# Low halves of weight tiles by an adding transfer instead of a VectorE subtraction, for two tiles of every eight

## The chip, the cores and the metric

The kernel runs on one core of one Trainium2 chip. The metric is the device time of one execution in microseconds. A core has a matrix engine (TensorE, PE in the profile), VectorE (DVE), ScalarE (ACT), GpSimd (POOL) and SyncE (SP), each with an instruction queue of its own that is worked through in order, and sixteen DMA engines that move data between DRAM and the on-chip memory, or within the latter. Instructions of different engines wait for one another by semaphores. A DMA can be issued from SP's, ScalarE's or GpSimd's queue.

## The reference

A trunk of two layers over 256 tokens of 2048 features, float32. Layer 0 mixes tokens with an mLSTM (8 heads), layer 1 with a Griffin block (convolution of width 4 and a gated linear recurrence). After each mixer comes a feed-forward block with 5632 inner features, and a final norm ends it:

```python
for layer in range(DEPTH):
    hn = rms_norm(h, norm_mix[layer])
    mix = mlstm_mixer(...) if layer % 2 == 0 else rglru_mixer(...)
    h = h + mix
    h = h + swiglu(rms_norm(h, norm_ffn[layer]), ffn_w_in[layer], ffn_w_out[layer])
return rms_norm(h, norm_final)
```

What matters here is only that nearly all the work is products `x @ w` of 256 tokens with large weight matrices: the mixers' input and output projections, and `ffn_w_in` (2048 x 11264) and `ffn_w_out` (5632 x 2048) of each layer. Every weight is used once.

## The kernel before, in words

The products must have nearly float32 precision. TensorE multiplies in a faster 32-bit format that keeps fewer bits (float32r). So each weight and each activation is split in two: a high half, which is the value rounded to float32r, and a low half, which is the value minus its high half. A product is then high x high + high x low + low x high.

The weights come in tiles of 256 rows x 512 columns (512 KB): 128 partitions, two row blocks, `NB` = 512 columns. `load_raw` (its DMA is line 77 of the profile) issues the load of such a tile on SP's queue into the buffer `raw`. The generator `stream` then has ScalarE copy `raw` into `whi`, rounding to float32r (line 161), and VectorE subtract `whi` from `raw` into `wlo` (line 162). It yields the row blocks one after the other to the product loops `linear_tok` (products in lines 176 to 178), `linear_feat` (through `mm_feat`, lines 193 to 195) and `linear_wide` (lines 217 and 218); in all of them the product with `wlo` is the second or third of a row block. A whole run has 752 such tiles: 96 of `m_w_in`, 32 of `m_w_out`, 352 of `ffn_w_in`, 176 of `ffn_w_out`, 64 of `r_w_in` and 32 of `r_w_out`. The first four tiles are loaded ahead of the program (`raw0`; the first of them in two halves); `stream` calls these `first`.

`raw`, `whi` and `wlo` each have four buffers (`wpool`, `bufs=4`): a buffer is written anew when all readers of the tile four places before are done. The scheduler orders each engine's instructions by priority; the split runs under `tc.high_priority(offset=AHEAD)`, so that it is placed as early as the buffers allow:

```python
with tc.high_priority(offset=0 if first else AHEAD):
    for i in range(0, 2, step):
        r = raw[:, i:i + step, 0:ncols]
        nc.scalar.copy(hi[:, i:i + step, 0:ncols], r)
        nc.vector.tensor_tensor(lo[...], r, hi[...].bitcast(F32), op=ALU.subtract)
```

The eight gate weight tiles of layer 1 (`gr`, loaded in line 614) share the `raw`, `whi` and `wlo` buffers and are split by `split_store` (lines 318 and 319).

GpSimd has little to do: 62 instructions, among them the reciprocal roots of the norms (line 291) and of the mLSTM heads (line 489), the scaling of the heads (line 490), and in the last feed-forward the product of h with the final gain (line 698). It issues no DMA. The results of one phase are worked on by the other engines between the products of the next (`pending`, `run_pending`).

Of the kernel before, what the change touches and what calls it, by code (L numbers as in the profile page):

```python
# [11 lines left out]
ALU = mybir.AluOpType  # L12
PSUM = bass.MemoryType.PSUM

P = 128
T = 256
# [15 lines left out]
def kernel(  # L32
# [21 lines left out]
    nc = tc.nc  # L54
# [10 lines left out]
    def misc(name):  # L65
        return ps_m.tile([P, NB], F32, tag="misc", name=name)

# [1 line left out]
    h = const.tile([P, NT, D], F32, name="h")  # L69
    xv = x[0].rearrange("(b p) d -> p b d", p=P)  # L70
    raw0 = {}
# [12 lines left out]
                for kg in (4 * q, 4 * q + 2):  # L84
                    raw0[kg] = load_raw(m_w_in[0], 0, NB, kg, 1 if kg == 0 else 2)

# [1 line left out]
    ident = const.tile([P, P], F32, name="ident")  # L88
    make_identity(nc, ident)
    ones = const.tile([P, P], F32, name="ones")  # L90
    nc.vector.memset(ones, 1.0)
    warm = const.tile([P, 1], F32, name="warm")
    nc.scalar.activation(warm, ones[:, 0:1], AF.Exp)
    # the tensor engine's clock rises only while it works
    pwarm = misc("warm")
    for i in range(12):
        nc.tensor.matmul(pwarm[:, 0:P], lhsT=ones, rhs=ones, start=(i == 0), stop=(i == 11))
# [6 lines left out]
        pattern=[[1, P]], channel_multiplier=-1,  # L104
    )

# [1 line left out]
    par_src = [  # L108
        ("g_mix", norm_mix.rearrange("l (k p) -> (l k) p", p=P), 32),
        ("g_ffn", norm_ffn.rearrange("l (k p) -> (l k) p", p=P), 32),  # L110
# [7 lines left out]
    rows = [const.tile([P, P], F32, name=f"rows{i}") for i in range(3)]  # L118
# [20 lines left out]

    par_cols(0)  # L140

# [1 line left out]
    pending = []  # L143

    def run_pending():
        if pending:
            pending.pop(0)()

# [1 line left out]
    def stream(w, c0, nk, ncols=NB):  # L150
        """Yields (k, hi, lo) for the 128-row tiles of w[:, c0:c0+ncols]."""
        for kg in range(0, nk, 2):
            first = kg in raw0
            raw = raw0.pop(kg) if first else load_raw(w, c0, ncols, kg)
            hi = wpool.tile([P, 2, NB], F32R, tag="whi", name=f"whi{kg}")
            lo = wpool.tile([P, 2, NB], F32R, tag="wlo", name=f"wlo{kg}")
            step = 1 if first and kg == 0 else 2
            with tc.high_priority(offset=0 if first else AHEAD):
                for i in range(0, 2, step):
                    r = raw[:, i:i + step, 0:ncols]  # L160
                    nc.scalar.copy(hi[:, i:i + step, 0:ncols], r)  # L161
                    nc.vector.tensor_tensor(  # L162
                        lo[:, i:i + step, 0:ncols], r, hi[:, i:i + step, 0:ncols].bitcast(F32), op=ALU.subtract
                    )
            for i in range(2):
                yield kg + i, hi[:, i, 0:ncols], lo[:, i, 0:ncols]

    def linear_tok(w, c0, nk, act, name, ncols=NB, lag=0):
        """[tokens, ncols] in PSUM, one tile for each block of 128 tokens."""
        ps = [acc(f"{name}_{b}") for b in range(NT)]  # L170

        def block(b, k, hi, lo):
            ah, al = act(k)
            bs = slice(b * P, (b + 1) * P)
            o = ps[b][:, 0:ncols]
            nc.tensor.matmul(o, lhsT=ah[:, bs], rhs=hi, start=(k == 0), stop=False)  # L176
            nc.tensor.matmul(o, lhsT=ah[:, bs], rhs=lo, start=False, stop=False)  # L177
            nc.tensor.matmul(o, lhsT=al[:, bs], rhs=hi, start=False, stop=(k == nk - 1))  # L178

        late = []  # L180
        for k, hi, lo in stream(w, c0, nk, ncols):
            block(0, k, hi, lo)
            late.append((k, hi, lo))
            if len(late) > lag:
                block(1, *late.pop(0))
            if k > 1:
                run_pending()
        for kt in late:
            block(1, *kt)
        return ps  # L190
# [4 lines left out]
        nc.tensor.matmul(o, lhsT=lo, rhs=ah, start=False, stop=last, skip_group_check=True)  # L195

    def linear_feat(w, c0, nk, act, name):
        """[features, tokens] in PSUM: two tiles of two blocks of 128 features."""
        ps = [acc(f"{name}_{b}").rearrange("p (f t) -> p f t", f=2) for b in range(2)]
        for k, hi, lo in stream(w, c0, nk):  # L200
            ah, al = act(k)
            for f in range(4):
                fs = slice(f * P, (f + 1) * P)
                mm_feat(ps[f // 2][:, f % 2, :], hi[:, fs], lo[:, fs], ah, al,
                        k == 0 and f % 2 == 0, k == nk - 1)
            if k > 1:
                run_pending()
        return ps

    def linear_wide(w, c0, nk, act, act2, name):  # L210
        """Four tiles of 128 features: columns 0:T and T:2T are to be added to get [features, tokens]."""
        ps = [acc(f"{name}_{f}") if f < 2 else misc(f"{name}_{f}") for f in range(4)]
        for k, hi, lo in stream(w, c0, nk):
            ah, _ = act(k)
            for f in range(4):
                fs = slice(f * P, (f + 1) * P)
                nc.tensor.matmul(ps[f], lhsT=hi[:, fs], rhs=act2(k), start=(k == 0), stop=False, skip_group_check=True)  # L217
                nc.tensor.matmul(ps[f][:, 0:T], lhsT=lo[:, fs], rhs=ah, start=False, stop=(k == nk - 1),  # L218
                                 skip_group_check=True)
            if k > 1:  # L220
                run_pending()
        return ps
# [6 lines left out]
    def bc4(ap):  # L229
        return ap.unsqueeze(1).broadcast_to([P, 4, T])  # L230

# [1 line left out]
    class Norm:  # L233
        lag = 0

# [66 lines left out]
        return ap.unsqueeze(1).broadcast_to([P, 2, T])  # L302

    def project_out(w, nk, act, nxt):
        """h += act.T @ w, and the next norm's operands, by quarters."""
        for q in range(4):
            ps = linear_tok(w, q * NB, nk, act, f"po{q}", lag=nxt.lag if q == 3 else 0)
            for b in range(NT):
                hs = h[:, b, q * NB:(q + 1) * NB]
                nc.vector.tensor_tensor(hs, ps[b], hs, op=ALU.add)  # L310
                if q == 3 and nxt.lag:
                    nxt.store(b)
            if q < 3 or not nxt.lag:
                pending.append(lambda q=q: nxt.done(q))

    def split_store(dst_hi, dst_lo, src):
        """The two halves of src (SBUF or PSUM), of the same shape."""
        nc.scalar.copy(dst_hi, src)
        nc.vector.tensor_tensor(dst_lo, src, dst_hi.bitcast(F32), op=ALU.subtract)

    def log1p_exp_nabs_half(pool, xin, shape, name):
        """log1p(exp(-|x|)) / 2, by the series of atanh."""
        e = pool.tile(shape, F32, name=f"{name}_e", tag=f"{name}_e", bufs=1)
        nc.scalar.activation(e, xin, AF.Abs)
        nc.scalar.activation(e, e, AF.Exp, scale=-1.0)
        s = pool.tile(shape, F32, name=f"{name}_s", tag=f"{name}_s", bufs=1)
# [5 lines left out]
        p = pool.tile(shape, F32, name=f"{name}_p", tag=f"{name}_p", bufs=1)  # L332
# [3 lines left out]
        nc.vector.scalar_tensor_tensor(out=p, in0=p, scalar=1.0, in1=s, op0=ALU.add, op1=ALU.mult)  # L336
        return p

    # =============================== layer 0: mLSTM ===============================
    n0 = Norm("m0", par["g_mix"][:, 0:16], bcast=True)  # L340
    for q in range(4):
        n0.quarter(q)
# [2 lines left out]
    def mlstm_mixer():  # L345
        with tc.tile_pool(name="mx", bufs=2) as mx:
            w = m_w_in[0]
            sel = mx.tile([H, H, P], F32R, name="sel", bufs=1)
            nc.gpsimd.tensor_copy(sel, ident[0:H, 0:H].unsqueeze(2).broadcast_to([H, H, P]))
            # gates  # L350
            gw = mx.tile([P, NK, 2 * H], F32, name="gw", bufs=1)
            nc.sync.dma_start(gw, w.rearrange("(k p) n -> p k n", p=P)[:, :, 6144:6160])
            gwx = mx.tile([P, NK, 2, 2 * H], F32R, name="gwx", bufs=1)
# [27 lines left out]
            def gate_rows():  # L381
# [9 lines left out]
                nc.vector.tensor_scalar_min(fg, fg, 0.0)  # L391
                lf = fg
                nc.vector.scalar_tensor_tensor(out=lf, in0=lp, scalar=-2.0, in1=fg, op0=ALU.mult, op1=ALU.add)
                # sums of log forget gates and running maxima, in blocks of 128 tokens
                cs = mx.tile([H, T], F32, tag="lf_e", name="cs", bufs=1)
                one8 = ones[0:H, :]
                for b in range(NT):
# [21 lines left out]

            pending.append(gate_rows)  # L420

            # q and k, features on partitions
            qT = mx.tile([P, H, T], F32, name="qT", bufs=1)
            kT = mx.tile([P, H, T], F32, name="kT", bufs=1)
            pw = []
# [84 lines left out]
            for j in range(4):  # L510
# [18 lines left out]
                hi = mx.tile([P, 4, T], F32R, tag=f"yh{j}", name=f"yh{j}", bufs=1)  # L529
                lo = mx.tile([P, 4, T], F32R, tag=f"yl{j}", name=f"yl{j}", bufs=1)  # L530
# [5 lines left out]

    mlstm_mixer()

    # =============================== feed-forward ===============================
    def ffn(layer, n, nxt):  # L540
        with tc.tile_pool(name=f"ff{layer}", bufs=2) as fp:
            w = ffn_w_in[layer]
# [19 lines left out]
    n2 = Norm("m1", par["g_mix"][:, 16:32], bcast=True)  # L562
    ffn(0, n1, n2)

    # =============================== layer 1: RG-LRU ===============================
    # 8 * softplus(-a)
    ap = par["a"]
    lpa = log1p_exp_nabs_half(const, ap, [P, NK], "spa")
    sp8 = const.tile([P, NK], F32, name="sp8")
# [7 lines left out]
    def rglru_mixer():  # L577
        with tc.tile_pool(name="rg", bufs=1) as rg:
            w = r_w_in[0]
# [26 lines left out]

            def gates(j):
                rv, rvh, rvl = rvs[j], rvhs[j], rvls[j]
                # gates of the two blocks of 256 channels
                r = rg.tile([P, 4, T], F32, tag="r", name=f"r{j}")  # L610
                ii = rg.tile([P, 4, T], F32, tag="ii", name=f"ii{j}")
                for g in range(2):
                    raw = wpool.tile([P, 2, NB], F32, tag="raw", name=f"gr{j}{g}")
                    nc.sync.dma_start(raw, gwv[:, 4 * j + 2 * g:4 * j + 2 * g + 2, :])
                    hi = wpool.tile([P, 2, NB], F32R, tag="whi", name=f"ghi{j}{g}")
                    lo = wpool.tile([P, 2, NB], F32R, tag="wlo", name=f"glo{j}{g}")
                    split_store(hi, lo, raw)
                    for half, dst in ((0, r), (1, ii)):
# [6 lines left out]
                        for f in range(2):  # L625
# [1 line left out]
                            nc.scalar.activation(  # L627
                                dst[:, 2 * g + f, :], pg[:, f, :], AF.Sigmoid, bias=par["gb"][:, gb:gb + 1]
                            )
                # log a = -8 softplus(-a) r;  1 - a^2 = tanh(-log a) (1 + a^2)  # L630
                th = rg.tile([P, 4, T], F32, tag="th", name=f"th{j}")
                for f in range(4):
                    k = 4 * j + f
# [49 lines left out]

    rglru_mixer()

    # =============================== last feed-forward, final norm ===============================
    class Final(Norm):
        lag = 4

# [62 lines left out]
```

## Time and profile before

| | |
|---|---|
| median of 2 runs | 2186.55 us |
| the two runs | 2191.62 and 2181.48 us |
| span of the profiled execution | 2190.3 us |
| TensorE busy | 2177.1 us (99%) |
| weight loads (PEld) | 1890.9 us (86%) |
| VectorE | 1272.6 us (58%) |
| ScalarE | 1053.6 us (48%) |
| GpSimd | 44.2 us (2%) |
| read from DRAM | 401.84 MB |

The time of the profiled execution is not listed by itself; its span, from the first to the last instruction, is 1.3 us shorter than the slower of the two runs and 8.8 us longer than the faster. In the rows of the profile, a group of instructions has its line in the program, the engine, the operation, the written and the read tiles, the count, the busy time, the mean duration in nanoseconds, and after the second bar the engine's idle time just before them with what ended it. A row of waits says which engine and line waited for which, then the total in microseconds, how often, and the longest. Rows of the timeline begin with the start and the duration in microseconds. PE's matmuls overlap one another, so a busy TensorE is not one at its peak rate.

### The profile page before, as it was taken

The page shows a single profiled execution, that of the slowest core. Times are in us where ns is not written, and L with a number is a line of the kernel's source. Part 1 is how long each engine was busy: PE and PEld are TensorE (multiplying, and loading weights), DVE is VectorE, ACT ScalarE, POOL GpSimd, SP SyncE. Part 2 cuts the span into 40 slices and gives each one's busy share as a digit, 9 for nine tenths or more (in the row PEclk, how much of TensorE's full clock was granted, in tenths as well). Part 3 has the DMA queues.
Part 4 walks back from the last instruction along what each step waited for, and adds up shares of the span by engine and source line. Part 5 has one row for each costly group of instructions (what it writes and reads, how often), then busy time and mean ns, then how long its engine had stood idle before and what let it go on. Part 6 is the DMA issues. An engine that isn't in the chain of part 4 may idle for free.

```text
span 2190.3 us, 30308 instructions
## 1 busy us (share of the span) xinstructions
PE 2177.1 (99%) x12092; PEld 1890.9 (86%) x12092; DVE 1272.6 (58%) x1452; ACT 1053.6 (48%) x1334; POOL 44.2 (2%) x62
## 2 busy tenths in 40 slices
PE   9999999999999999999999999999999999999998
PEld 8988888888888888888889999888888888888886
DVE  6655555556565666544445786655656566554444
ACT  5344544545444444444445648544445444444433
POOL 0011110000000000000000000000000000000000
PEclk9999999999999999999999999999999999999999
DMA  6556655666666666555566665566666666665554
GB/s 207 164 163 183 180 177 183 183 192 187 190 191 191 187 191 192 191 187 189 189 186 183 184 183 183 183 180 186 185 190 184 186 188 184 188 206 192 192 183 154
DMA packets 211094, 405.92 MB, mean 185 GB/s; under 512 B 14520, under 2 KB 14728, under 8 KB 210824
## 3 DMA queue, kind: packets, MB, share of 16 engines
q1 hardware_dynamic: 210808, 402.94, 60.6%
q8 instruction: 94, 1.54, 0.3%
q10 hardware_dynamic: 144, 1.05, 0.1%
q14 instruction: 48, 0.39, 0.0%
HBM read 401.84 MB, written 2.10 MB: 184 GB/s over the span
## 4 chain that ended last, share of the span: by engine, by line
PE 98%; ACT 0%; DVE 0%; DMA 0%; issue 0%; SPq 0%; ACTq 0%; POOLq 0%; POOL 0%
PE u L217 15%; PE g L217 15%; PE po L178 10%; PE po L177 10%; PE po L176 10%; PE u L218 8%; PE g L218 8%; PE qk L193 1%; PE qk L195 1%; PE qk L194 1%; PE rec L193 1%; PE rec L195 1%; PE rec L194 1%; PE gb L195 1%; PE gb L194 1%; PE gb L193 1%
## 5 line engine op out<-in xcount | busy, mean ns | idle before, releaser
L162 DVE TENSOR_TENSOR wlo<-raw,whi 128x1024 fp32r<-128x1024 f32 (+1 forms) x753 | 921.7, 1225 | 858.2 <-ACT whi L161 857.7
L161 ACT CAST whi<-raw 128x1024 fp32r<-128x1024 f32 (+1 forms) x753 | 790.2, 1050 | 1006.3 <-PE po L178 359.9
L217 PE MATMUL g<-x_f,whi 128*128 128x512 f32 x1408 | 494.0, 395 | 0.0
L217 PE MATMUL u<-x_f,whi 128*128 128x512 f32 x1408 | 493.8, 395 | 0.0
L218 PE MATMUL g<-x_f,wlo 128*128 128x256 f32 x1408 | 395.2, 281 | 0.0
L218 PE MATMUL u<-x_f,wlo 128*128 128x256 f32 x1408 | 394.8, 280 | 0.0
L217 PEld LDWEIGHTS u<-x_f,whi 128*128 128x128 f32 x1408 | 263.9, 187 | 61.9
L217 PEld LDWEIGHTS g<-x_f,whi 128*128 128x128 f32 x1408 | 263.9, 187 | 61.7
L178 PE MATMUL po<-whi,hl 128*128 128x512 f32 x704 | 276.3, 392 | 0.0
L176 PE MATMUL po<-whi,hh 128*128 128x512 f32 x704 | 275.3, 391 | 0.0
L177 PE MATMUL po<-wlo,hh 128*128 128x512 f32 x704 | 275.1, 391 | 0.0
L218 PEld LDWEIGHTS g<-x_f,wlo 128*128 128x128 f32 x1408 | 266.0, 189 | 0.1
L218 PEld LDWEIGHTS u<-x_f,wlo 128*128 128x128 f32 x1408 | 266.0, 189 | 0.0
L177 PEld LDWEIGHTS po<-wlo,hh 128*128 128x128 f32 x704 | 132.2, 188 | 29.6
L178 PEld LDWEIGHTS po<-whi,hl 128*128 128x128 f32 x704 | 132.3, 188 | 28.4
L176 PEld LDWEIGHTS po<-whi,hh 128*128 128x128 f32 x704 | 132.2, 188 | 28.4
L193 PE MATMUL qk<-x_m,whi 128*128 128x256 f32 x256 | 74.2, 290 | 3.3 <-ACT x_m L264 3.3
L195 PE MATMUL qk<-x_m,wlo 128*128 128x256 f32 x256 | 73.4, 287 | 0.0
L194 PE MATMUL qk<-x_m,whi 128*128 128x256 f32 x256 | 73.2, 286 | 0.0
L193 PE MATMUL rec<-x_m,whi 128*128 128x256 f32 x256 | 72.6, 284 | 0.0
L195 PE MATMUL gb<-x_m,wlo 128*128 128x256 f32 x256 | 72.5, 283 | 0.0
L193 PE MATMUL gb<-x_m,whi 128*128 128x256 f32 x256 | 72.5, 283 | 0.0
(219 smaller groups left out, 2473.7 us busy)
## 6 DMA issues: line engine op xcount, KB each, us to landing
raw<-in_ffn_w_in_dram SPq DMA_DIRECT2D x352, 512.0 KB, 3.7
raw<-in_ffn_w_out_dram SPq DMA_DIRECT2D x176, 512.0 KB, 3.6
raw<-in_m_w_in_dram SPq DMA_DIRECT2D x95, 512.0 KB, 3.8
raw<-in_r_w_in_dram SPq DMA_DIRECT2D x64, 512.0 KB, 3.8
raw<-in_m_w_out_dram SPq DMA_DIRECT2D x32, 512.0 KB, 3.6
raw<-in_r_w_out_dram SPq DMA_DIRECT2D x32, 512.0 KB, 3.6
gr<-in_r_gate_w_dram SPq DMA_DIRECT2D x8, 512.0 KB, 4.1
h<-in_x_dram SPq DMA_DIRECT2D x4, 512.0 KB, 7.8
```

The source lines that it names most:

```text
L161: nc.scalar.copy(hi[:, i:i + step, 0:ncols], r)
L162: nc.vector.tensor_tensor(lo[:, i:i + step, 0:ncols], r, hi[:, i:i + step, 0:ncols].bitcast(F32), op=ALU.subtract)
L176: nc.tensor.matmul(o, lhsT=ah[:, bs], rhs=hi, start=(k == 0), stop=False)
L177: nc.tensor.matmul(o, lhsT=ah[:, bs], rhs=lo, start=False, stop=False)
L178: nc.tensor.matmul(o, lhsT=al[:, bs], rhs=hi, start=False, stop=(k == nk - 1))
L193: nc.tensor.matmul(o, lhsT=hi, rhs=ah, start=first_in_bank, stop=False, skip_group_check=True)
L194: nc.tensor.matmul(o, lhsT=hi, rhs=al, start=False, stop=False, skip_group_check=True)
L195: nc.tensor.matmul(o, lhsT=lo, rhs=ah, start=False, stop=last, skip_group_check=True)
L217: nc.tensor.matmul(ps[f], lhsT=hi[:, fs], rhs=act2(k), start=(k == 0), stop=False, skip_group_check=True)
L218: nc.tensor.matmul(ps[f][:, 0:T], lhsT=lo[:, fs], rhs=ah, start=False, stop=(k == nk - 1), skip_group_check=True)
```

## The change

`stream` counts the weight tiles. For the tiles with a count of 3 or 7 modulo 8, `first` ones excepted, VectorE's subtraction is left out. Instead ScalarE reads `raw` a second time and writes it, multiplied by -1 and rounded to float32r as in `whi`, to `wlo`: the negative of the high half. Then a DMA issued from GpSimd's queue adds the raw values to `wlo`, which gives raw minus high half, the same low half. With a count of 3 the source of the transfer is the raw tile on the chip, with a count of 7 it is the weight matrix in DRAM, which is read there a second time. The rest of the diff takes out comments.

```diff
+    turn = [0]
+
     def stream(w, c0, nk, ncols=NB):
         for kg in range(0, nk, 2):
...
             step = 1 if first and kg == 0 else 2
+            turn[0] += 1
+            way = turn[0] % 8 if not first else 0
             with tc.high_priority(offset=0 if first else AHEAD):
                 for i in range(0, 2, step):
                     r = raw[:, i:i + step, 0:ncols]
                     nc.scalar.copy(hi[:, i:i + step, 0:ncols], r)
+                    if way in (3, 7):
+                        nc.scalar.mul(lo[:, :, 0:ncols], r, -1.0)
+                        src = r
+                        if way == 7:
+                            src = w.rearrange("(k p) n -> p k n", p=P)[:, kg:kg + 2, c0:c0 + ncols]
+                        nc.gpsimd.dma_start(lo[:, :, 0:ncols], src, accum_op=ALU.add)
+                        continue
                     nc.vector.tensor_tensor(
                         lo[:, i:i + step, 0:ncols], r, hi[:, i:i + step, 0:ncols].bitcast(F32), op=ALU.subtract
                     )
```

## The prediction

> **What bounds the kernel now.** I read the page's shares and slices first, then the chain that ended last.
>
> ```profile
> PE 2177.1 (99%) x12092; PEld 1890.9 (86%) x12092; DVE 1272.6 (58%) x1452; ACT 1053.6 (48%) x1334; POOL 44.2 (2%) x62
> ...
> PEclk9999999999999999999999999999999999999999
> DMA  6556655666666666555566665566666666665554
> ...
> q1 hardware_dynamic: 210808, 402.94, 60.6%
> ...
> PE 98%; ACT 0%; DVE 0%; DMA 0%; issue 0%; SPq 0%; ACTq 0%; POOLq 0%; POOL 0%
> ```
>
> TensorE is busy 2177.1 of the 2190.3 us span, at the highest clock digit in every slice, and the chain is 98% TensorE. At most 13.2 us of idle time is there to be won. VectorE, which the change relieves, is busy 58% and has no share in the chain. So the only open question is whether a low half made the new way reaches TensorE in time. The waits of TensorE's weight loads show that today it does:
>
> ```profile
> PEld po L177 <- DVE wlo L162: 0.8, 2, 0.5
> ```
>
> Two waits on VectorE's low half in 752 tiles, 0.8 us in all. How much room there is must be read from one stretch of the feed-forward, ScalarE's and VectorE's rows (start, duration, what ended the idle time):
>
> ```profile
> 801.01 1.05 ACT L161 CAST whi<-raw 128x1024 fp32r<-128x1024 f32 x1 [1.72 <-PE u L217]
> ...
> 809.33 1.06 ACT L161 CAST whi<-raw 128x1024 fp32r<-128x1024 f32 x1 [1.41 <-PE g L217]
> 812.11 1.06 ACT L161 CAST whi<-raw 128x1024 fp32r<-128x1024 f32 x1 [1.72 <-PE g L217]
> ```
> ```profile
> 802.10 1.23 DVE L162 TENSOR_TENSOR wlo<-raw,whi 128x1024 fp32r<-128x1024 f32 x1 [1.55 <-ACT whi L161]
> ```
> ```profile
> 1011.66 1.05 ACT L161 CAST whi<-raw 128x1024 fp32r<-128x1024 f32 x1 [1.69 <-PE po L178]
> 1014.41 1.05 ACT L161 CAST whi<-raw 128x1024 fp32r<-128x1024 f32 x1 [1.70 <-PE po L178]
> 1017.15 1.05 ACT L161 CAST whi<-raw 128x1024 fp32r<-128x1024 f32 x1 [1.70 <-PE po L178]
> ```
>
> From 801.01 to 812.11 lie four tiles, 2.775 us each; in the output projection the step is 2.745. I take T = 2.76 us for one tile of TensorE work. Each cast is ended by TensorE: with four buffers per tag it starts when TensorE has left tile n-4. Then TensorE works through three more tiles, so the low half of tile n is wanted 3T = 8.28 us after its cast began (it is the second product of a row block). Today it is there after 802.10 + 1.23 - 801.01 = 2.32 us: 5.96 us to spare.
>
> **The change part by part.** The counter runs over 752 tiles (751 whole ones and one made in halves). Remainder 3 comes 94 times, one of them a first tile that keeps the old way: 93 with the raw tile as source. Remainder 7 comes 94 times, with the weights read again from DRAM. Together 187.
>
> ```profile
> L162 DVE TENSOR_TENSOR wlo<-raw,whi 128x1024 fp32r<-128x1024 f32 x751 | 920.3, 1226 | 851.0 <-ACT whi L161 850.5
> ```
> ```profile
> L161 ACT CAST whi<-raw 128x1024 fp32r<-128x1024 f32 x751 | 788.9, 1051 | 1005.6 <-PE po L178 359.9 <-PE u L217 231.7 <-PE g L217 221.2
> ```
>
> Removed: 187 subtractions of 1.226 us, 229 us of VectorE, worth nothing on the path. Added on ScalarE: 187 scaled copies; this form of the multiplication is not in the trace, the nearest row is the cast, 1.05 us, so 196 us, which takes ScalarE from 48% to 57%. Its idle time before casts, 1005.6 us, covers that; what it costs is latency within the tile.
>
> Now the latency L of a new low half, from the start of its cast. Cast and scaled copy one behind the other: 2.10 us; hand-over 0.04 us (802.10 less 802.06): 2.14. Then GpSimd issues the transfer. No transfer is issued by GpSimd in this trace. Its cost is bounded below by SP's issue of a load and above by GpSimd's longest row:
>
> ```profile
> L77 SPq DMA_DIRECT2D raw<-in_ffn_w_in_dram x352: 367/368/368, 387.8 to 1919.6; - x176
> ...
> DMA to landing us min/median/max: 3.4/3.7/9.5
> ```
> ```profile
> L490 POOL TENSOR_SCALAR hn<-hn,den 128x256 f32<-128x256 f32 x16 | 14.8, 930 | 0.8
> L489 POOL TENSOR_TENSOR den<-den,mhalf 128x1 f32<-128x1 f32 x16 | 12.1, 767 | 249.5 <-DVE den L485 249.5
> L698 POOL TENSOR_TENSOR y<-h,gf 128x512 f32<-128x512 f32 x6 | 10.6, 1793 | 669.6 <-DVE h L310 669.6
> ```
>
> Between 0.37 and 1.79 us I take 0.93, GpSimd's own commonest larger instruction: L is 3.07 at the issue's end. A load of the same 512 KB lands 3.7 us after its issue began, 3.7 - 0.37 = 3.33 after it ended: 6.40. An adding transfer also has to read what it adds to. What one pass over 512 KB costs: 60.6% of 2190.3 us is 1327 us for 402.94 MB, or 768.5 times 0.524 MB: 1.73 us of all sixteen engines. Bounds for the addition are nothing (the second read beside the first) and four passes; I take one more pass: 8.13. Last, loads already hold the engines 60.6% of the time. The transfer meets between no load and two; I take half a load, 0.87. **L = 9.00 us**, with ends 2.14 + 0.37 + 3.33 = 5.84 and 2.14 + 1.79 + 3.33 + 3 x 1.73 + 2 x 1.73 = 15.9.
>
> The Trainium skill's page "Collectives: The Full Stack" (Part 3, on why reduce-scatter is half of all-gather) says of adding transfers that the sum itself is free but two source reads go through one ring, at half the copy rate. No row here shows an addition; by that rule the extra term is one pass, as taken above.
>
> Every such tile stalls TensorE by L - 3T = 9.00 - 8.28 = 0.72 us. In the 93 tiles whose source is the raw tile there is a second effect. SP's queue now waits almost only for the subtraction to free the raw buffer:
>
> ```profile
> SPq L77 <- DVE wlo L162: 1535.7, 641, 7.1
> ```
>
> Behind the transfer, that buffer is free at 9.00 instead of 2.32. The load for tile n+4 then lands at 9.00 + 3.7 = 12.70, while TensorE asks ScalarE for that tile at 4T + 0.72 = 11.76: 0.94 us late. Tile n+4 is always one of the other kind (remainder 7 follows 3 by four), so its own 9.00 us start 0.94 later and it stalls 0.72 + 0.94 = 1.66. Loads n+5 to n+7 stand behind n+4 on SP and go out in a bunch, but ordinary tiles have 5.96 us to spare. The DRAM kind frees its raw buffer at 2.14 and hands no delay on.
>
> Sum: 93 x 0.72 = 67, 94 x 1.66 = 156, together 223 us; on the profiled execution's 2190.3 us, **2413 us**. The two runs shown are 2181.48 and 2191.62, so the span is 3.8 us above their median, and a change under 2% (44 us) could hardly be told from none here.
>
> GpSimd's other 62 instructions now share a queue with 187 triggers that wait for ScalarE. Behind a waiting trigger stand the reciprocal roots of the norms and heads, for which VectorE's broadcast and then TensorE wait; there are four norms and 16 head rows, each can lose an issue or a wait, some 1 to 3 us, mostly under other products. The other way round:
>
> ```profile
> POOL den L489 <- DVE den L485: 249.5, 8, 127.8
> ```
>
> a trigger placed behind such a long wait (up to 127.8 us) would hold up TensorE. The rows are independent of weights and get ready in the order of the program, so I cost this at nothing, up to 20 x 3 = 60 us.
>
> **The rivals.** *Hidden.* The transfer lands as a load does, the second read hidden: L = 6.40, the next raw tile at 10.10, before 11.04. Nothing stalls, and the time is 2190. For it: the 5.96 us to spare. Against it: GpSimd, the addition and the engines' load all come on top of ScalarE's second pass. It decides at L = 4T - 3.7 = 7.34; up to L = 7.81 the 94 late loads cost 94 x 0.47 = 44 us, still within 2%. The Trainium skill's page "DMA: Bandwidth & Descriptors" (Anatomy of one DMA) speaks for it: about 2.0 us plus bytes over 436 GB/s for a GpSimd-issued transfer, an estimated 3.2 us for 512 KB, so that L would be some 5.3 us; no run here shows such a transfer alone.
>
> *The DMA engines become the bound.* Four loads are 6.91 us of the 11.04 us that four tiles take, so an addition may use 4.13 us before they fill up. At a quarter of a load's rate it takes 6.91, four tiles take 13.82, and 187 x 2.78 = 520 us come on top: 2710 us. For it: 60.6% are taken already, in every slice (digits 5 and 6). Against it: that slow a rate has no row.
>
> *Faster.* VectorE's 229 us less could let TensorE's waits at the phase ends go. They are 13.2 us in all, so 2177 us, under 1%; a gain of over 2% would need a cheaper product, and nothing touches the products.
>
> **How the numbers follow.** My forecast, stalls from L between 7.81 and 10.3: 0.50; alone it spans 2234 (44 us) to 2656 (93 x 2.02 + 94 x 2.96 = 466 us). Hidden or within 2%: 0.29. DMA bound, from about 2650 up: 0.19. Faster by over 2%: 0.02. The range reaches from the hidden case with the spread of the runs, 2180, to 2680, part of the way into the DMA-bound case; some 0.15 is left above and little below. Slower is 0.50 + 0.19 = 0.69, same 0.29, faster 0.02.
>
> **What the changed profile would show.** Right: TensorE's busy share near 2177 / 2413 = 90%; weight loads waiting for a DMA on wlo about 187 times, mean 1.2 us; ScalarE waiting for late raw loads some 94 times; GpSimd rows of about 0.9 us; VectorE near 1044 us busy, ScalarE near 1250. Wrong if the transfer lands under 5 us from GpSimd's start (hidden), or if the DMA digits stand at 9 and ordinary loads land far later than 3.7 us (DMA bound). If TensorE waits but on few tiles for long, the order of GpSimd's queue is the cause.

## The result and the profile after

The changed kernel takes 2423.65 us (median of two runs, 2413.72 and 2433.58) against 2186.55: a ratio of 1.1078, 95% interval 1.0951 to 1.1204, slower by 11%. The prediction was 2413 us. The total is close, but it is made up of other terms than those of the sum, as the profile shows.

The page of the changed kernel, the rows that answer to those of before:

```profile
PE 2237.1 (92%) x12092; PEld 1917.8 (79%) x12092; DVE 1047.8 (43%) x1265; ACT 1223.7 (50%) x1521; POOL 238.2 (10%) x249
...
PEclk8999999999999999999999999999999999999998
DMA  6777767778777787777777767677878787877764
...
q1 hardware_dynamic: 210808, 402.94, 51.5%
q0 software_dynamic: 38960, 98.05, 22.8%
...
PE 57%; DMA 34%; ACT 4%; issue 3%; POOL 1%; DVE 1%; SPq 0%; ACTq 0%; POOLq 0%
...
L174 DVE TENSOR_TENSOR wlo<-raw,whi 128x1024 fp32r<-128x1024 f32 (+1 forms) x566 | 692.4, 1224 | 963.9 <-ACT whi L165 963.6
...
L168 ACT ACTIVATE wlo<-raw 128x1024 fp32r<-128x1024 f32 x187 | 197.6, 1057 | 174.8 <-PE po L189 135.0
```

The chain that ended last is no longer TensorE alone: 34% of it is DMA. VectorE's subtractions lost their 229 us and ScalarE got its 187 scaled copies, as counted. (From line 161 on, line numbers are 4 to 12 higher than before.) The span grew by 2431.6 - 2190.3 = 241.3 us, and it splits in two: TensorE's idle time rose from 13.2 to 194.5 us (181 more), and its busy time from 2177.1 to 2237.1 (60 more) for the same 12092 products.

Which transfers TensorE waited for, from the list of waits (engine, line and tile waiting, then the releaser; total us, times, longest):

```profile
PE po L189 <- DMA wlo<-in_ffn_w_out_dram: 48.8, 22, 5.7
...
PE u L230 <- DMA wlo<-in_ffn_w_in_dram: 38.9, 22, 2.8
...
PE g L230 <- DMA wlo<-in_ffn_w_in_dram: 36.3, 22, 2.5
...
PE po L189 <- DMA wlo<-raw: 7.2, 3, 4.4
```

Over all matrices there are 94 such waits with 181 us: 91 of them, 174 us, for transfers that read DRAM, and 3 for those that read the raw tile on the chip. So the loss sits in one of the two kinds. The transfers' own rows, for the time in GpSimd's queue (min/median/max) and then the median from issue to landing:

```profile
L172 POOL DMA_DIRECT2D wlo<-raw x93: 892/901/927, 46.5 to 2397.6; - x93
L172 POOL DMA_DIRECT2D wlo<-in_ffn_w_in_dram x44: 1203/1203/1265, 453.5 to 2122.7; - x44
```
```profile
wlo<-raw POOLq DMA_DIRECT2D x93, 512.0 KB, 4.7
...
wlo<-in_ffn_w_in_dram POOLq DMA_DIRECT2D x44, 512.0 KB, 8.0
wlo<-in_ffn_w_out_dram POOLq DMA_DIRECT2D x22, 512.0 KB, 9.1
```

The on-chip kind lands in 4.7 us, the DRAM kind in 8 to 9. One of each, from the timeline of the feed-forward:

```profile
899.53 1.05 ACT L165 CAST whi<-raw 128x1024 fp32r<-128x1024 f32 x1 [0.87 <-ACT hh L330]
900.49 1.05 ACT L168 ACTIVATE wlo<-raw 128x1024 fp32r<-128x1024 f32 x1
...
914.87 1.05 ACT L165 CAST whi<-raw 128x1024 fp32r<-128x1024 f32 x1 [5.86 <-PE g L229]
```
```profile
901.83 1.20 POOL L172 DMA_DIRECT2D wlo<-in_ffn_w_in_dram  x1 [10.40 <-ACT wlo L168]
917.18 0.90 POOL L172 DMA_DIRECT2D wlo<-raw  x1 [14.14 <-ACT sg L238]
```

In the on-chip kind the low half is there 917.18 - 914.87 + 4.7 = 7.0 us after its cast began, ahead of the 8.28 us at which it is wanted. In the DRAM kind it is 2.30 + 8.0 = 10.3 us. The chain of waits has the DRAM transfer as "901.83 8.88 DMA", so it landed at 910.71, and TensorE stood still:

```profile
907.89 0.39 PE L229 MATMUL g<-x_f,whi 128*128 128x512 f32 x1
910.76 0.58 PE L230 MATMUL g<-x_f,wlo 128*128 128x256 f32 x1 [2.48 <-DMA wlo<-in_ffn_w_in_dram]
911.13 0.63 PE L229 MATMUL g<-x_f,whi 128*128 128x512 f32 x1
```

The same product takes 0.39 us before the wait and 0.63 after it: TensorE's granted clock was 0.50 from 910.8 to 913.6 and 1.00 before and after. That is where the 60 us of additional busy time come from for the most part; more below. (In 36 of the 93 on-chip tiles, those of the output projections above all, ScalarE makes the scaled copy first, and the low half is there 6.0 us after ScalarE began with the tile.)

Why does the DRAM kind take 3.3 us longer? The DMA queues in those two flights, first the DRAM one (901.8 to 910.7), then the on-chip one (917.2 to 921.9); columns are packets, MB, share of the sixteen engines:

```profile
q1 hardware_dynamic: 809, 1.54, 54.0%
q0 software_dynamic: 272, 0.52, 35.1%
```
```profile
q0 software_dynamic: 144, 0.52, 62.3%
q1 hardware_dynamic: 32, 0.07, 9.7%
```

Beside the DRAM transfer SP's ordinary loads (q1) moved 1.54 MB, three tiles; beside the on-chip one almost nothing. There SP's queue stood still, first for a subtraction of VectorE and then for the very raw buffer that this transfer was reading: the load behind it went out at 921.88, as the transfer landed. In the whole kernel SP waited for such transfers 91 times, 4.4 us in the mean:

```profile
SPq L77 <- DMA wlo<-raw: 396.4, 91, 11.2
```

I call load work the time of the load packets between a transfer's issue and its last packet, divided by sixteen engines. Counted from the trace's packets, its median is 0.0 us for the on-chip kind and 3.8 us for the DRAM kind (1.9 us of it ahead of the transfer's first packet). The first packet of a DRAM transfer starts 2.6 us after the issue (1.5 us on chip), and from the first to the last one 5.0 us pass (2.5 us), though the transfer needs only 3.06 us of all engines.

How do the two queues share an engine? Two stretches of the same flight, without loads (905 to 907) and with them (908.5 to 910.5):

```profile
q0 software_dynamic: 153, 0.31, 95.1%
...
q1 hardware_dynamic: 2, 0.00, 0.1%
```
```profile
q1 hardware_dynamic: 310, 0.60, 90.2%
q0 software_dynamic: 16, 0.02, 6.9%
```

The second stretch looks as if the loads crowded the transfer out, but by then only 12 of its 256 data packets were left, and the last eight started 157 to 158 ns and then 250 to 252 ns apart, one behind the other. Over all 94 DRAM flights two distances between the starts of adding packets stand out: 157 to 158 ns (with its multiples), which is back to back, and 250 to 251 ns, which leaves room for one load packet of 84 ns between them. Nothing stands out near 343 ns, where two load packets would fit. The trace does not name the engine of a packet, but these distances are those of an engine that takes one packet of each queue in turn. The Trainium skill, "DMA: Bandwidth & Descriptors" (Queues, rings and completion order), says that an engine takes the rows it has work for in turn, a packet each; the distances agree. So the loads do not shut the transfer out. They make it later by the load work that stands ahead of it and between its packets.

### The profile page after: what moved, and what is told of

Its sections match the earlier page's. It is cut to its first block, busy times and chain, and to the rows that moved or that the text cites. A ratio compares the mean times of both kernels' runs of the same rounds, so it can differ in the third digit from the quotient of the medians.

```text
span 2431.6 us, 30670 instructions
## 1 busy us (share of the span) xinstructions
PE 2237.1 (92%) x12092; PEld 1917.8 (79%) x12092; DVE 1047.8 (43%) x1265; ACT 1223.7 (50%) x1521; POOL 238.2 (10%) x249
## 3 DMA queue, kind: packets, MB, share of 16 engines
q1 hardware_dynamic: 210808, 402.94, 51.5%
q0 software_dynamic: 38960, 98.05, 22.8%
q8 instruction: 94, 1.54, 0.3%
q10 hardware_dynamic: 144, 1.05, 0.1%
## 4 chain that ended last, share of the span: by engine, by line
PE 57%; DMA 34%; ACT 4%; issue 3%; POOL 1%; DVE 1%; SPq 0%; ACTq 0%; POOLq 0%
DMA wlo<-in_ffn_w_in_dram 14%; PE u L229 9%; PE g L229 9%; DMA wlo<-in_ffn_w_out_dram 8%; PE po L189 6%; PE u L230 5%; PE po L190 5%; PE po L188 5%; PE g L230 5%; DMA wlo<-in_m_w_in_dram 3%; DMA wlo<-in_r_w_in_dram 3%; ACT wlo L168 2%; DMA wlo<-raw 2%; DMA wlo<-in_m_w_out_dram 1%; DMA wlo<-in_r_w_out_dram 1%
## 5 line engine op out<-in xcount | busy, mean ns | idle before, releaser
L174 DVE TENSOR_TENSOR wlo<-raw,whi 128x1024 fp32r<-128x1024 f32 (+1 forms) x566 | 692.4, 1224 | 963.9 <-ACT whi L165 963.6
L229 PE MATMUL u<-x_f,whi 128*128 128x512 f32 x1408 | 502.1, 399 | 0.0
L229 PE MATMUL g<-x_f,whi 128*128 128x512 f32 x1408 | 499.1, 397 | 0.0
L230 PE MATMUL u<-x_f,wlo 128*128 128x256 f32 x1408 | 400.9, 285 | 38.9 <-DMA wlo<-in_ffn_w_in_dram 38.9
L189 PE MATMUL po<-wlo,hh 128*128 128x512 f32 x704 | 282.2, 401 | 51.6 <-DMA wlo<-in_ffn_w_out_dram 48.8
L168 ACT ACTIVATE wlo<-raw 128x1024 fp32r<-128x1024 f32 x187 | 197.6, 1057 | 174.8 <-PE po L189 135.0
L190 PE MATMUL po<-whi,hl 128*128 128x512 f32 x704 | 279.6, 397 | 0.0
L188 PE MATMUL po<-whi,hh 128*128 128x512 f32 x704 | 279.0, 397 | 0.0
L172 POOL DMA_DIRECT2D wlo<-raw x93 | 83.9, 902 | 1149.6 <-ACT wlo L168 668.1
L190 PEld LDWEIGHTS po<-whi,hl 128*128 128x128 f32 x704 | 134.9, 192 | 29.4
L188 PEld LDWEIGHTS po<-whi,hh 128*128 128x128 f32 x704 | 134.4, 191 | 29.3
L172 POOL DMA_DIRECT2D wlo<-in_ffn_w_in_dram x44 | 53.1, 1206 | 452.0 <-ACT wlo L168 441.0
L207 PE MATMUL rec<-x_m,wlo 128*128 128x256 f32 x256 | 74.9, 293 | 11.2 <-DMA wlo<-in_r_w_in_dram 11.2
L239 DVE TENSOR_TENSOR v<-u,v 128x256 f32<-128x256 f32 x88 | 33.2, 419 | 116.1 <-ACT v L238 116.1
```

What stands on the lines that cost most here:

```text
L168: nc.scalar.mul(lo[:, :, 0:ncols], r, -1.0)
L172: nc.gpsimd.dma_start(lo[:, :, 0:ncols], src, accum_op=ALU.add)
L174: nc.vector.tensor_tensor(lo[:, i:i + step, 0:ncols], r, hi[:, i:i + step, 0:ncols].bitcast(F32), op=ALU.subtract)
L239: nc.vector.tensor_tensor(dst[:, f, :], ps[f][:, 0:T], dst[:, f, :], op=ALU.add)
```

## The experiments

Times without an interval are single runs; the kernel before took 2186 to 2191 us (medians) beside them.

**Only on-chip transfers** (all 187 read the raw tile).

```diff
-                        if way == 7:
+                        if False:
                             src = w.rearrange(...)
```

> All 187 adding transfers take the on-chip raw tile as source, none reads the weights again from DRAM. In the changed kernel TensorE's waits for a DMA are 174 us on the DRAM kind and 7 us on the on-chip kind. Theory 1 (the DRAM kind alone is late): the on-chip kind is there about 2.3 us + 4.7 us = 7.0 us after its cast began, before the 8.3 us at which it is wanted, so the stalls and the half-clock stretches go and the time is 2190 to 2210 us. Theory 2 (the raw buffer handed on late, the second term of the prediction): buffer free at 7.0 us, next load 3.7 to 4.7 us, so a group of four tiles needs 10.7 to 11.7 us against 11.04 us; at the upper end every group loses 0.66 us, 187 x 0.66 = 123 us, and the time is about 2310 us.

Measured: 2213.28 us, ratio 1.0110, interval 1.0073 to 1.0147. Landing 4.9 us, 9 waits of TensorE with 13 us, mean clock 0.997 as before. Taking DRAM out as the source removes nine tenths of the loss, so the kind of source decides. The time lies 3 us above theory 1's range and far below theory 2's 2310. The handed-on delay exists, but it is small:

```profile
ACT wlo L168 <- DMA raw<-in_ffn_w_out_dram: 26.2, 13, 2.8
```

ScalarE waited 13 times for a late raw tile in this kernel, and the spare time of the tile took most of it.

**Raw buffer held** until the DRAM transfer has landed, so that SP cannot issue the next load beside it.

```diff
                         nc.gpsimd.dma_start(lo[:, :, 0:ncols], src, accum_op=ALU.add)
+                        if way == 7:
+                            hold = small.tile([P, 1], F32, tag="hold", name="hold")
+                            nc.gpsimd.tensor_tensor(hold, raw[:, 0, 0:1], lo[:, 0, 0:1].bitcast(F32), op=ALU.add)
```

> As the changed kernel, but in the DRAM kind a one-element GpSimd addition reads raw and wlo behind the transfer, so that the raw buffer is not free, and the next load not issued, until the transfer has landed. Theory 1a (the DRAM kind is late because ordinary loads run ahead of it and beside it, 1.9 + 2.0 us of them in the trace): it lands about 5 us instead of 8 us after its issue, the low half is there at 7.5 us, TensorE's waits on DMA fall from 181 us to under 40 us, and the time is 2200 to 2280 us. Theory 1b (reading DRAM in 2 KB pieces with an addition is slow by itself): landing stays near 8 us and the time is 2430 us or more, since the raw buffer is now held as well.

Measured: 2266.8 us. This edit only adds work and waits, and yet it saves 157 us, because fewer loads run ahead of the transfer and beside it (load work of 1.1 us in the median instead of 3.8):

```profile
wlo<-in_ffn_w_in_dram POOLq DMA_DIRECT2D x44, 512.0 KB, 6.0
wlo<-in_ffn_w_out_dram POOLq DMA_DIRECT2D x22, 512.0 KB, 6.0
```

8.0 and 9.1 us became 6.0, and TensorE's DMA waits fell from 181 to 47 us. That is theory 1a, though the landing came to 6 and not 5 us: a part of the difference is not the loads'. (The on-chip kind has as much load work in this run, 1.0 us, and lands in 4.9 us.) Here the raw buffer is handed on late from both kinds, and ScalarE's waits show it (124.8 us in 35 waits for ffn_w_out).

**Negative half first** in the program.

```diff
-                    nc.scalar.copy(hi[:, i:i + step, 0:ncols], r)
                     if way in (3, 7):
                         nc.scalar.mul(lo[:, :, 0:ncols], r, -1.0)
+                    nc.scalar.copy(hi[:, i:i + step, 0:ncols], r)
```

> As the changed kernel, but ScalarE writes the negative high half before the high half in the 187 tiles, so that the transfer is issued 1.05 us earlier. If the stall is the low half's latency less three tiles of TensorE work, each of the some 90 stalls (mean 1.9 us) gets up to 1.05 us shorter: about 90 us less waiting, fewer half-clock stretches, so 2310 to 2350 us. If the wait comes from a fixed order of queues or from loads that go first whenever the transfer is issued, nothing is won and it stays at 2400 to 2430 us.

Measured: 2423.14 us, no difference, but it decides nothing: in the feed-forward's input products ScalarE's rows still have the cast first, presumably because `whi` comes free before `wlo` and the scheduler orders by readiness; in the output projections (L188 to L190) the scaled copy was first already in the changed kernel. So the order was forced:

```diff
+                        neg = nc.scalar.mul(lo[:, :, 0:ncols], r, -1.0)
+                        with tc.issue_after(neg.ins):
+                            nc.scalar.copy(hi[:, i:i + step, 0:ncols], r)
```

> As the changed kernel, but in the 187 tiles ScalarE's queue has the negative high half ahead of the high half by an order edge (the kernel that only wrote it first in the program kept the cast first in the feed-forward's input products). There the transfer goes out some 0.8 to 1.0 us earlier; in the output projections the order is that already. If the stall is latency less lead, the 44 stalls of ffn_w_in, the 8 of r_w_in and 4 of m_w_in lose 0.8 us each, 45 us and some half-clock stretches: 2360 to 2390 us. If the transfer only meets the loads earlier and lands at the same time: 2415 to 2430 us.

Measured: 2502.45 us, slower by 79 us, which neither side expected. The transfer does go out earlier: its issue comes 1.36 us after ScalarE's first row of the tile instead of 2.30.

```profile
935.46 1.06 ACT L166 ACTIVATE wlo<-raw 128x1024 fp32r<-128x1024 f32 x1 [0.88 <-PE g L233]
```
```profile
936.82 1.20 POOL L175 DMA_DIRECT2D wlo<-in_ffn_w_in_dram  x1 [10.19 <-ACT wlo L166]
```
```profile
wlo<-in_ffn_w_in_dram POOLq DMA_DIRECT2D x44, 512.0 KB, 9.9
```

But it lands 9.9 us after its issue instead of 8.0. Its load work is 5.5 us (3.7 in the changed kernel; medians of the 44 flights of ffn_w_in). TensorE's DMA waits rose to 208 us, and the half-clock stretches from 110 to 195 us. So "latency less lead" with a fixed latency is wrong for this kind: what counts is the load work that the flight meets. Why the earlier issue meets that much more load work is not settled.

**4 KB pieces from DRAM** (the DRAM kind reads 128 rows of 1024 adjacent columns, so other weights than the tile's).

```diff
-    src = w.rearrange("(k p) n -> p k n", p=P)[:, kg:kg + 2, c0:c0 + ncols]
+    cc = min(c0, w.shape[1] - 2 * NB)
+    src = w.rearrange("(k p) n -> p k n", p=P)[:, kg, cc:cc + 2 * NB].rearrange("p (k n) -> p k n", k=2)
```

> As the changed kernel, but the DRAM kind reads 128 rows of 1024 adjacent columns (4 KB pieces, the same 512 KB, other weights than the tile's) instead of 256 rows of 512 (2 KB pieces). Theory 1b (piece size): issue falls from 1.20 to about 0.90 us, landing from 8 us towards 5 us, time 2200 to 2300 us. Theory 1a (loads ahead and beside): landing falls by no more than the 0.3 us of issue and about 0.3 us of engine time, time 2360 to 2420 us.

Measured: 2328.03 us, between the two ranges. Landing 7.1 us, DMA waits 92 us. Piece size has a share: issue takes 0.86 instead of 1.20 us, and 0.9 us off the landing takes half of the waits, since they were 1.9 us each. The load work remains (3.2 us in the median), and so does a landing 2.5 us above the on-chip kind's.

**Both together.**

> The two that helped the DRAM kind, together: 4 KB pieces (other weights than the tile's) and the raw buffer held until the transfer has landed. By itself the first left 92 us of DMA waits and the second 47 us, of 181. If both act on the same lateness and the DRAM read itself has no price of its own, the DRAM kind now lands within 5.3 us of its issue like the on-chip kind and the time is that of the kernel with 187 on-chip transfers, 2205 to 2225 us. If reading DRAM with an addition has a price of its own, landing stays at 6 us or more and the time above 2240 us.

Measured: 2238.3 us, between the two ranges and just below the upper; landing 6.0 us (ffn_w_in) and 5.5 (ffn_w_out), DMA waits 34 us. The two help together, but the landing stays about 1 us above the on-chip kind's 4.8 in this run (load work of 1.1 us for the one and 1.0 for the other), so reading DRAM seems to have a price that neither removes.

**Only the DRAM kind** (`if way == 7`), and **all 187 from DRAM** (`if True` for the source).

> Only the 94 tiles of the DRAM kind go the new way; the 93 of the on-chip kind are split by VectorE as before. Theory 1a (each DRAM transfer is held up by loads that its own tile and its neighbours set free): the loss of 241 us stays but for some 10 to 25 us that the on-chip kind costs, 2400 to 2425 us. Rival (the on-chip kind holds a raw buffer, SP's queue stands behind it, and the bunch of loads that then goes out is what the next DRAM transfer meets, the prediction's hand-on in another form): without it the landing falls well below 8 us and the time below 2350 us.

> All 187 transfers read DRAM. In the changed kernel the 94 of this kind cost (2431.6 - 2190.3) / 94 = 2.57 us each. Theory 1a: the cost doubles with the count, 2190 + 187 x 2.57 = 2670 us, say 2600 to 2700. Rival (bunched loads behind the on-chip kind): without that kind each costs less, under 2500 us.

Measured: 2395.88 and 2500.22 us. Without any on-chip transfer the DRAM kind lands after 7.8 us (ffn_w_in) and 9.0 (ffn_w_out), hardly sooner, and the time falls by 28 us, little more than the 20 us between the two runs of the changed kernel and just outside the 2400 to 2425 us of theory 1a: bunched loads behind the on-chip kind are not the cause. With all 187 from DRAM the cost does not double: (2498.4 - 2190.3) / 187 = 1.65 us per transfer, and the 165 waits average 1.47 us instead of 1.91. Theory 1a's 2600 to 2700 was too high, and the time stands at the edge of the rival's range, which the run with the DRAM kind alone rules out. What fell per transfer is the load work, to 3.2 us in the median from 3.8 (3.6 with the DRAM kind alone), and half-clock stretches fell to 62 us in all; a likely reason is that the more frequent stalls stretch the time over which the same loads are spread.

**No addition** (the DRAM kind's transfer overwrites, so that its low half is the whole value).

```diff
-   nc.gpsimd.dma_start(lo[:, :, 0:ncols], src, accum_op=ALU.add)
+   nc.gpsimd.dma_start(lo[:, :, 0:ncols], src, accum_op=ALU.add if way == 3 else ALU.bypass)
```

> The DRAM kind's transfer writes the raw values over wlo instead of adding them (the low half is then wrong in these 94 tiles); all else as in the changed kernel. The addition's second read is 1.5 of the 3.06 us of engine time that such a transfer takes. If it counts as one more pass: engine time near 1.6 us, landing 8.0 - 1.5 = 6.5 us or less, TensorE waiting 94 x (1.9 - 1.5) = 40 us or less, 2230 to 2290 us. If the addition is free and the wait comes from loads alone: landing 7.5 to 8 us, 2390 to 2430 us.

Measured: 2235.3 us; landing 5.1 us (ffn_w_in) and 6.9 (ffn_w_out), DMA waits 24 us. The second read is a full pass: a 2 KB packet of the transfer takes 178 ns with the addition and 99 without (medians), a whole transfer 3.06 and 1.65 us of all engines, and the issue shrank from 1.20 to 0.71 us. The shorter transfer also meets less load work, 2.9 us instead of 3.8 (medians).

**2 KB pieces on the chip** (`max_dma_last_dim=2048`, all 187 on-chip).

> As the kernel with 187 on-chip transfers (2213 us), but in pieces of at most 2 KB, 256 instead of 128 of them. It shows what the pieces cost without DRAM and without loads beside them. Theory 1a: issue 0.9 to 1.2 us, engine time 2.8 to 3.0 us, landing 4.9 to 5.3 us, and the raw buffer is handed on 0.4 us later; 2215 to 2290 us. Theory 1b (small adding pieces are slow by themselves): landing 7 us or more, and since every tile hands its raw buffer on late, over 2400 us.

Measured: 2222.71 us, landing 5.3 us. Small pieces alone cost 9 us over the median of the same kernel with 4 KB pieces (6 us over its slowest run); theory 1b is out.

**Only the on-chip kind, 93 tiles** (`if way == 3`).

> Only the 93 tiles of the on-chip kind go the new way, none from DRAM. 187 of them cost 22.8 us. If each costs the same: 2190.5 + 11 = 2202 us. If the cost comes from the raw buffer handed from one such tile to the next, four tiles on (the second term of the prediction), the chain is broken when they stand eight apart: 2186 to 2195 us, no difference from before. VectorE is relieved of 114 us; if that were worth anything the time would be below 2185 us.

Measured: 2198.41 us against 2190.41, ratio 1.0034, interval 1.0009 to 1.0060; 4 waits with 4 us. Some 8 us for 93 and 23 for 187: the on-chip kind costs about 0.1 us apiece, nearer the even price than the chain. VectorE's 112 us less brought nothing. No version here beats the kernel before.

## Why the prediction came out right, point by point

- *TensorE bounds the kernel, VectorE's relief is worth nothing.* Shown: the 93 on-chip tiles and the 187 take 0.3% and 1.1% more time with 112 and 224 us less VectorE work.
- *Counts and engine costs.* 93 and 94, 187 scaled copies of 1.057 us (1.05 taken), VectorE 1047.8 us (1044), ScalarE 1223.7 (1250; cast and copy overlap by 0.1 us). GpSimd's issue was 0.90 and 1.20 us (0.93), within its bounds; the hand-over to GpSimd, taken as 0.04 us from VectorE's row, was 901.83 - 901.54 = 0.29.
- *One more pass for the addition.* Right in kind and nearly in size: 1.41 us (3.06 less 1.65) against 1.73. The Trainium skill's rule in "Collectives: The Full Stack" (Part 3), half the copy rate for two source reads, agrees roughly: a 2 KB packet takes 178 ns with the addition, 99 without it, and 84 in a load.
- *Half a load, 0.87 us, of contention for both kinds.* This is the step that failed. The on-chip kind meets almost no load (0.0 us of load work in the median), as its own raw buffer is not free for a load when it starts: in 40 of the 93 flights SP issued no load before the landing, in 53 one, some 2.8 us after the transfer's issue. The DRAM kind frees its buffer before it is even issued and meets 3.8 us. In place of L = 9.00 for both, the runs show 7.0 (6.0 where the scaled copy comes first) and 10.3 us. A second term was too large: the load's 3.33 us and the extra pass of 1.73 us, 5.06 us behind the issue, took 4.7 - 0.9 = 3.8 us on chip.
- *Stalls of 93 x 0.72 and 94 x 1.66.* In fact 3 waits and 91 with a mean of 1.91. The 67 us of the on-chip kind did not come. The 156 us of the other did (174), but from its own lateness, not from 0.94 us handed on: with the on-chip kind gone, 154 us of the waits remained. The hand-on failed for two reasons. Its condition, L over 7.34, was not met. And the step took for granted that SP loads tile n+4 into the buffer that tile n holds. In 53 of the 93 cases that load waited for a later tile's subtraction instead, and the buffer that the transfer held went to tile n+5, an ordinary one. Together, the load of tile n+4 was issued 5.1 us after the cast of tile n began and had landed at 8.9 us (medians; 11.0 at the latest), before the 11.04 us at which it is wanted, though a load took 4.7 us here instead of 3.7. Late raw tiles show up with 187 on-chip tiles (26 us of ScalarE's waits for ffn_w_out) and with the buffer held (125 us).
- *Left out: the clock.* 60 us came from TensorE's busy time. The trace has 110 us at half clock instead of 15, and half of the additional 96 is 48 us of lost work. That the sum came within 1% is therefore in part luck: two terms that did not come, 67 and 88, stand against a longer DRAM wait and the clock.
- *The rivals.* Hidden would have been right for on-chip sources alone, at 4.7 us to landing. The Trainium skill's fit in "DMA: Bandwidth & Descriptors" (Anatomy of one DMA), an estimated 3.2 us, names no addition and is too low for this transfer. The DMA engines did not become the bound: 51.5% + 22.8% of them are in use, and the digits stay at 6 to 8 up to the last slice. What bounded was the latency of a DRAM transfer with load work ahead of it and beside it. The order of GpSimd's queue left no mark: no wait in the lists points to it; it was not tried by itself.
- *The signs in the profile.* TensorE's share is 92% (90 forecast). In place of 187 waits with a mean of 1.2 us there are 94 with 1.9, and in place of some 94 waits of ScalarE for late raw tiles there are 7. The sign of the hidden case, landing under 5 us, is met by the on-chip kind.

## What to carry to other kernels

When work is moved to a transfer, ask which other transfers will be running in its flight, and what releases them: holding a buffer back paid here, because it kept the next load out of the way. Whether a deadline is met depends on the load work in that one flight, not on a mean share of the DMA engines: 3 us of transfer work took 8 us with 3.8 us of load work, and 6 us with 1.1. Where one engine is busy 99% of the time, as here, relieving another one had nothing to win.

## What the runs showed of the hardware that was not expected

- SP's loads and GpSimd's adding transfer take turns on a DMA engine, packet by packet, as far as the distances between packets show it: 250 ns from one adding packet of 2 KB to the next with a load packet between them, 158 without. Still, a transfer with a deadline of three tiles is late by it.
- An adding transfer costs 2.1 times a load per packet (178 to 84 ns at 2 KB), with source and destination both on the chip too (340 to 159 ns at 4 KB).
- A wait of TensorE for a DMA can halve its clock for a stretch of 3.413 us (in 24 of 134 cases twice that). Waits for DMA in the changed kernel and six of the experiments (those with 50 waits or more), and how many had a half-clock stretch that began in the wait or within 3.5 us behind it:

```
wait          waits   with a half-clock stretch
under 2 us      514    29
2 to 2.5 us      61    27
over 2.5 us      91    78
```

Whether a wait has one depends on where it falls. In each of these runs the stretches begin on a fixed grid of 3.413 us. By TensorE's rows (the start and the end of the kernel left out), all 134 follow a grid interval in which it was idle for 1.61 us or more, and every interval with more than 1.92 us of idle time was followed by half clock.

The Trainium skill, "TensorE: Matmul & The Clock Gate" (Part 1), has the half rate set in after an idle window of about 3.4 us. The length of the stretches agrees, but about half of such a stretch idle was enough here.
